# Element-wise work of a streaming encoder step moved from GpSimd to VectorE

## The chip, the cores and the metric

One core of one Trainium2 chip. The metric is device time in microseconds of the whole program, from launch to end; lower is better. A core has five engines with queues of their own, each working in order: TensorE (PE: matmuls, and PEld: loads of its weights), VectorE (DVE), ScalarE (ACT), GpSimd (POOL) and SyncE (SP, which here only issues DMAs).

## What is computed

One inference step of a two-layer encoder on 512 prompt tokens and 64 sample tokens, in float32, width 1024. Cut to what matters here:

```python
def rmsnorm(x, g):
    return x * rsqrt(mean(x * x, axis=-1) + 1e-6) * g

def trunk_layer(x, ...):
    h = rmsnorm(x, g_mix_norm)
    proj = h @ w_in                       # split into qa ka va | qg kg vg ag rg | cq ckv kr
    o_a = rmsnorm(stick_breaking_attention(qa, ka, va))
    o_b, gla_s = gla_recurrence(qg, kg, vg, log_a, s0)
    o_b = rmsnorm(o_b) * silu(rg)         # the retrieval gate
    o_c = rmsnorm(mla_attention(cq, ckv, kr))
    x = x + concat(o_a, o_b, o_c) @ w_out
    x = x + memory_cross_attention(rmsnorm(x, g_cross_norm), mem_k, mem_v)
    h = rmsnorm(x, g_ffn_norm)
    return x + (silu(h @ w_gate) * (h @ w_up)) @ w_down

...

# gla_recurrence, each block of 16 tokens
S = exp(b_last) * S + kd.T @ v            # the state, 4 heads of 32 x 64
```

## The kernel before

All 576 tokens are worked at once, in five token tiles (four of 128 and one of 64). The residual stream X lies transposed in SBUF, eight blocks of 128 features by 576 tokens. Each float32 matmul is made of three with split operands: a high part (wH, hH; written by ScalarE) and a low part (wL, hL; value minus high part, written by VectorE). Most operations go through one recording helper, so in the profile they all have line 209, and instructions are told apart by the tiles that they write and read. Tile names carry the stage: `win` the input projection, `gla` gated attention, `sb` stick-breaking attention, `wout` the output projection, `cross`, `ffn`; the digit is the layer.

**The stream's norms** (class `XNorm`, line 480 on). `add(k)` is called once for each of the eight feature blocks, right behind the residual add that completes the block: ScalarE writes hH, VectorE hL, ScalarE the square of the block into a tile of tag `u` (three buffers), and the square of block k is added to the running sum. Seven adds make one norm; those of k = 1 to 6 are on GpSimd, that of k = 7 on VectorE. `add` is called in `wout` (both layers, for the cross attention's norm) and in `down` at the end of the feed-forward block of layer 0 (for the second layer's first norm). A matmul with a constant matrix then sums over features, and ScalarE makes the factor R of it. The norm of layer 0's first stage is computed otherwise.

**The masked values of gated attention** (`states` in `gla`). The update of the state over blocks of 16 tokens is made with matmuls whose right side holds the values of a head once for each of up to eight blocks, zero outside the block: `vm[token, block, :] = vg[token, :] * blk[token, block]`. For each token tile two head pairs are done, each in a buffer of tag `pt` (two buffers): the first head's product on GpSimd, the second one's on VectorE, then four matmuls of TensorE for the pair into accumulator `gla.S`. The fifth tile has 64 tokens and four blocks, so its products are 64x256 instead of 128x512. When all five tiles are in, `scans` runs eight scans on VectorE over the prompt's states (`gla.U`) and one over the sample's.

**The retrieval gate** (`ev` in `win`). VectorE scales the projection out of the accumulator by R into G, ScalarE takes its sigmoid, and GpSimd multiplies G by it; four times in a layer (two feature blocks by two token halves).

The order of the tasks of the mixer stage is written out by hand (`STEPS`): in each layer it says when a unit of the input projection (W), of the states (l), of the scans (m) and so on is emitted. The cross attention's tasks are ordered by a planner with costs for each engine, and the feed-forward block is in program order. From the emitted program, the framework's scheduler makes each engine's queue, taking what comes earlier in the program first as far as its own model has it ready. After that the queues are fixed.

Of the kernel before, what the change touches and what calls it, by code (L numbers as in the profile page):

```python
# [26 lines left out]
KD = D // 128  # L27
# [203 lines left out]
def tile_hybrid(ctx, tc, ins, outs):  # L231
    clock = tc.clock = Clock()
    nc = Engines(tc)
# [16 lines left out]
    def nm(s):  # L250
        uid[0] += 1
        return f"{phase[0]}.{s}_{uid[0]}"

    def big(dt=F32, name="b"):
        return clock.tile(bp.tile([128, BIGN], dt, tag="big", name=nm(name)), "big", 11)

    def big4(dt=F32, name="b"):
        return big(dt, name).rearrange("p (a t) -> p a t", t=T)
# [13 lines left out]
    def u(tag="u", name=None):  # L272
        pool = up if tag in ("u", "R") else turn["pool"]
        return clock.tile(pool.tile([128, T], F32, tag=tag, name=nm(name or tag), bufs=UB[tag]), tag, UB[tag])
# [11 lines left out]
    def ps_(tag):  # L286
        return clock.tile(pp.tile([128, 512], F32, tag=tag, name=nm(tag), bufs=PB[tag]), tag, PB[tag])

    def cst(shape, name, dt=F32):
        return const.tile(shape, dt, tag=name, name=name)  # L290
# [6 lines left out]
    def act(out, in_, func, **kw):  # L297
        name = TABLES.get(func)
        if name is not None and name != held["set"]:
            load = nc.scalar.preload_act_table_set(name).ins  # L300
            for i in held["users"]:
                behind(tc, load, i)
            held.update(set=name, load=load, users=[load])
        ins = nc.scalar.activation(out, in_, func, **kw).ins
        if name is not None:
            behind(tc, ins, held["load"])
            held["users"].append(ins)
# [7 lines left out]
    def tt(out, a, b, op, eng=None):  # L315
        (eng or nc.vector).tensor_tensor(out, a, b, op=op)
# [4 lines left out]
    MUL, ADD, SUB = ALU.mult, ALU.add, ALU.subtract  # L321
# [55 lines left out]
    blk = cst([128, 8], "blk")  # L377
# [34 lines left out]
    def load_w(src, kt, n, src2=None, by="m"):  # L412
        return split_w(fetch_w(src, kt, n, src2), by)
# [38 lines left out]
    def ws_steps(w, m0, kt, aH, aL, evac, halves=(0, 1), tag="D"):  # L452

        ph = phase[0]
        for a in halves:
            phase[0] = ph
            cs = slice(a * HF, (a + 1) * HF)
            d = ps_(tag)[:, 0:HF]
            for k in range(kt):
                mm3(d, w[0](k, m0, m0 + 128), w[1](k, m0, m0 + 128), aH(k)[:, cs], aL(k)[:, cs], k == 0, k == kt - 1)  # L460
            evac(a, cs, d)
            yield "d"
# [17 lines left out]
    class XNorm:  # L480
# [13 lines left out]
        def add(self, k):  # L494
            self.split(k, slice(0, T))
            s = u()
            act(s, X[:, k, :], AF.Square)
            if k:
                tt(s, s, self.acc, ADD, None if k == KD - 1 else nc.gpsimd)
            self.acc = s  # L500

        @property
# [433 lines left out]
    def layer(l, xn):  # L936
# [11 lines left out]
        def nat(c0, n, fn, fn2=None, c1=None, n1=0):  # L948

            w = load_w(wi[:, c0:c0 + n], KD, n, None if c1 is None else wi[:, c1:c1 + n1], by="k")  # L950
            n += n1
            for t, (r0, rn) in enumerate(TILES):
                ps = ps_("D")[:, 0:n]
                for k in range(KD):
                    mm3(ps[0:rn], xn.h(k)[:, r0:r0 + rn], xn.l(k)[:, r0:r0 + rn], w[0](k, 0, n), w[1](k, 0, n),
                        k == 0, k == KD - 1)
                x = fn(t, r0, rn, ps[0:rn])
                if fn2 is not None:
                    od.later(lambda a=(t, r0, rn, x): fn2(*a))
                yield "d"  # L960
# [90 lines left out]
        def win():  # L1051

            G = st["G"] = big4(name="G")
            vgx = st["vgx"] = big(name="vg")
            st["vg"] = vgx[:, 0:1280].rearrange("p (t c) -> p t c", c=256)
            st["vga"] = vgx[:, 1280:1360].rearrange("p (t c) -> p t c", c=16)
            st["ckv"] = vgx[:, 1360:2160].rearrange("p (t c) -> p t c", c=160)
            st["lat"] = big(F32R, name="lat")[:, 0:2176].rearrange("p (a t) -> p a t", t=1088)
            st["krn"] = turn["pool"].tile([128, 288], F32, tag="krn", name=nm("krn"), bufs=1).rearrange("p (t c) -> p t c", c=32)
            w = load_w(wi[:, 768:1024], KD, 256) if l else w_first  # L1060
            for a in range(2):
                for p in range(2):
                    yield from ws_steps(w, p * 128, KD, xn.h, xn.l,
                                        lambda a, cs, d: tt(G[:, p, cs], d, xn.R[:, cs], MUL), [a])

            yield from nat(1808, 160, ckv1, lambda t, r0, rn, ln: lat_T(ln, rn, r0), 1200, 96)
            od.event("qk")
            yield from nat(1024, 256, vg1)
            od.event("vg")
            od.add(lat_past(), name="S")  # L1070
            w = load_w(wi[:, 0:256], KD, 256)
            for p in range(2):
                yield from ws_steps(w, p * 128, KD, xn.h, xn.l, lambda a, cs, d: tt(oSB[p][:, cs], d, xn.R[:, cs], MUL))
            od.add(sb_past(), name="Z")
            w = load_w(wi[:, 256:512], KD, 256)
            for a in range(2):
                for p in range(2):
                    yield from ws_steps(w, p * 128, KD, xn.h, xn.l,
                                        lambda a, cs, d: tt(sbk[:, p, cs], d, xn.R[:, cs], MUL), [a])
                for t in ([0, 1], [2, 3, 4])[a]:  # L1080
                    od.later(lambda t=t: ka_out(t, *TILES[t]))
            yield from nat(512, 256, va1)
            od.event("va")
            yield "after glan"
            w = load_w(wi[:, 1296:1552], KD, 256)
            for p in range(2):
                def ev(a, cs, d):
                    tt(G[:, 2 + p, cs], d, xn.R[:, cs], MUL)
                    s = u()[:, 0:HF]
                    act(s, G[:, 2 + p, cs], AF.Sigmoid)  # L1090
                    tt(G[:, 2 + p, cs], G[:, 2 + p, cs], s, MUL, nc.gpsimd)
                yield from ws_steps(w, p * 128, KD, xn.h, xn.l, ev)
            od.event("rg")
            yield "after glan"
            st["cT"] = big4(F32R, name="cT")
            yield from nat(1552, 256, cq1, cq2)
            od.event("win")
# [194 lines left out]
        def gla():  # L1292
            G, vgx, vg, vga = (st[x] for x in ("G", "vgx", "vg", "vga"))
# [19 lines left out]
            for a in range(2):  # L1313
                cs = slice(a * HF, (a + 1) * HF)
# [20 lines left out]
            for h in range(4):  # L1335
                s = slice(32 * h, 32 * h + 32)
# [10 lines left out]
            def states(t, r0, rn):  # L1347

                if t == 0:
                    st["Uf"] = big(name="U")[:, 0:2112]  # L1350
                    st["U"] = st["Uf"].rearrange("p (d n) -> p d n", n=33)
                    nc.vector.memset(st["U"][:, :, 0:1], 0.0)
                nb = rn // 16
                pt = ps_("T")
                tr(pt[0:rn, 0:128], kdT[:, r0:r0 + rn])
                kd = u()[0:rn, 0:128]
                copyA(kd, pt[0:rn, 0:128])
                yield "S"
                ps = ps_("S")
                for hp in range(2):  # L1360
                    vm = pt4("vm").rearrange("p (h n d) -> p h n d", h=2, n=8)
                    for hh in range(2):
                        h = 2 * hp + hh
                        tt(vm[0:rn, hh, 0:nb, :], vg[0:rn, t, h * 64:h * 64 + 64].unsqueeze(1).broadcast_to([rn, nb, 64]),
                           blk[0:rn, 0:nb].unsqueeze(2).broadcast_to([rn, nb, 64]), MUL, nc.vector if hh else nc.gpsimd)
                    if hp:
                        clock.keep(ps)
                    yield
                    for hh in range(2):
                        h = 2 * hp + hh  # L1370
                        nc.tensor.matmul(ps[32 * h:32 * h + 32, 0:nb * 64], lhsT=kd[:, 32 * h:32 * h + 32],
                                         rhs=vm[0:rn, hh, 0:nb, :].rearrange("p n d -> p (n d)"), start=True, stop=True,
                                         tile_position=(0, 32 * h))
                src = ps[:, 0:nb * 64].rearrange("p (n d) -> p d n", d=64)
                copyA(st["U"][:, :, 1 + 8 * t:9 + 8 * t] if t < 4 else Us[:, :, 1:5], src)
# [461 lines left out]
```

## Time and profile before

| what | value |
|---|---|
| time before, median of 3 runs | 1680.31 us (1679.86 to 1680.92) |
| the profiled execution, its own time | 1681.31 us |
| its span, first to last instruction | 1679.5 us |
| granted TensorE clock, mean | 0.991 |
| TensorE busy | 1644.6 us (98%) |
| VectorE busy | 1208.1 us (72%) |
| ScalarE busy | 898.3 us (53%) |
| GpSimd busy | 213.1 us (13%) |

Busy shares are means over stages with different limits. An engine's idle time before an instruction is put down to what released that instruction; in the timeline it stands in brackets. The granted clock is a share of full speed: 1.00 is 2.4 GHz, 0.50 is 1.2 GHz. Ends of matmuls are modelled, and spans on GpSimd are rough.

### The profile page before, as it was taken

The numbers are of one execution on the slowest core, as the hardware profiler recorded it, in microseconds if no ns is written. First come the engines' busy times: TensorE is split into PE (matmuls) and PEld (weight loads), VectorE is DVE, ScalarE is ACT, GpSimd is POOL, SyncE is SP. The second block draws the span as 40 slices with busy tenths as digits, with TensorE's granted clock in tenths as the row PEclk, the third lists the DMA queues.
The fourth block names the chain that finished last, engine by engine and source line by source line (L and its number), as shares of the span: only waits on it lengthen the run. The fifth ranks groups of instructions, "written<-read, shape, count | busy, mean of one in ns | idle before, by whom it ended". The sixth has DMA issues, their size and how long they took to land.

```text
span 1679.5 us, 30904 instructions
## 1 busy us (share of the span) xinstructions
PE 1644.6 (98%) x12279; PEld 1537.0 (92%) x12279; DVE 1208.1 (72%) x2462; ACT 898.3 (53%) x1915; POOL 213.1 (13%) x303
## 2 busy tenths in 40 slices
PE   8999999999999999999999999999999999999998
PEld 7879788689999999999998889877999999999998
DVE  5746798875898777667567378988668877667663
ACT  6426688755664444344443467886566544344431
POOL 3323341020000000000134043400200000000000
PEclk9999999999999999999999999999999999999999
DMA  5312230022122232322223213201211332322221
GB/s 167 116 45 87 70 108 32 26 76 76 51 76 87 90 98 79 101 82 95 80 71 99 78 54 108 75 27 37 90 52 51 101 101 76 101 83 94 94 83 57
DMA packets 113648, 133.31 MB, mean 79 GB/s; under 512 B 10610, under 2 KB 95712, under 8 KB 113504
## 3 DMA queue, kind: packets, MB, share of 16 engines
q1 hardware_dynamic: 113120, 131.30, 24.6%
q8 instruction: 97, 1.59, 0.4%
q14 instruction: 47, 0.39, 0.1%
q0 software_dynamic: 352, 0.03, 0.0%
q10 hardware_dynamic: 32, 0.01, 0.0%
HBM read 123.64 MB, written 7.68 MB: 78 GB/s over the span
## 4 chain that ended last, share of the span: by engine, by line
PE 78%; DVE 10%; issue 4%; ACT 3%; POOL 2%; DMA 2%; POOLq 0%; ACTq 0%; DVEq 0%
PE ffn0.D L209 9%; PE ffn1.D L209 9%; PE ffn0.T L209 7%; PE ffn1.T L209 7%; PE ffn0.S L209 7%; PE ffn1.S L209 6%; PE win1.D L209 5%; PE win0.D L209 3%; PE wout1.D L209 2%; PE wout0.D L209 2%; PE cross1.D L209 2%; PE cross0.D L209 2%; PE cross0.T L209 1%; PE cross1.T L209 1%; PE mlap0.T L209 1%
## 5 line engine op out<-in xcount | busy, mean ns | idle before, releaser
L209 ACT ACTIVATE ffn1.wH<-ffn1.wraw 128x1024 fp32r<-128x1024 f32 x64 | 59.3, 927 | 116.5 <-PE ffn1.T L209 61.1
L209 ACT ACTIVATE ffn0.wH<-ffn0.wraw 128x1024 fp32r<-128x1024 f32 x64 | 59.3, 927 | 111.8 <-PE ffn0.T L209 60.7
L209 DVE TENSOR_TENSOR ffn0.sL<-ffn0.sum,ffn0.sH 128x1024 fp32r<-128x1024 f32 x40 | 48.8, 1221 | 39.7 <-ACT ffn0.sH L209 39.7
L209 DVE TENSOR_TENSOR ffn1.sL<-ffn1.sum,ffn1.sH 128x1024 fp32r<-128x1024 f32 x40 | 48.9, 1221 | 39.7 <-ACT ffn1.sH L209 39.6
L209 DVE TENSOR_TENSOR ffn0.wL<-ffn0.wraw,ffn0.wH 128x1024 fp32r<-128x1024 f32 x64 | 67.5, 1055 | 8.3 <-ACT ffn0.wH L209 7.6
L209 DVE TENSOR_TENSOR ffn1.wL<-ffn1.wraw,ffn1.wH 128x1024 fp32r<-128x1024 f32 x64 | 67.5, 1055 | 8.3 <-ACT ffn1.wH L209 7.6
L209 POOL TENSOR_TENSOR ffn0.u<-ffn0.u,ffn0.u 128x576 f32<-128x576 f32 x6 | 10.0, 1673 | 460.6 <-DVE ffn0.wL L209 453.6
L209 PE MATMUL ffn1.D<-ffn1.bT,ffn1.sH 128*128 128x288 f32 x320 | 65.3, 295 | 0.1
L209 PE MATMUL ffn0.D<-ffn0.bT,ffn0.sH 128*128 128x288 f32 x320 | 65.1, 295 | 0.2
L209 ACT ACTIVATE ffn0.sH<-ffn0.sum 128x1024 fp32r<-128x1024 f32 x40 | 42.2, 1055 | 21.1 <-PE ffn0.S L209 20.9
L209 ACT ACTIVATE ffn1.sH<-ffn1.sum 128x1024 fp32r<-128x1024 f32 x40 | 42.2, 1055 | 21.1 <-PE ffn1.S L209 20.9
L209 PEld LDWEIGHTS ffn0.D<-ffn0.bT,ffn0.sH 128*128 128x128 f32 x320 | 51.6, 189 | 0.9 <-ACT ffn0.part L209 0.9
L209 PEld LDWEIGHTS ffn1.D<-ffn1.bT,ffn1.sH 128*128 128x128 f32 x320 | 51.6, 189 | 0.8 <-ACT ffn1.part L209 0.4
L209 PE MATMUL win0.D<-win0.wH,in.hH 128*128 128x256 f32 (+1 forms) x160 | 47.8, 299 | 0.0
L209 PE MATMUL ffn0.D<-ffn0.bT,ffn0.sL 128*128 128x288 f32 x160 | 47.5, 297 | 0.0
L209 PE MATMUL ffn1.D<-ffn1.bT,ffn1.sL 128*128 128x288 f32 x160 | 47.5, 297 | 0.0
L209 PE MATMUL win0.D<-win0.wL,in.hH 128*128 128x256 f32 (+1 forms) x160 | 46.8, 292 | 0.3 <-DVE win0.wL L209 0.3
L209 PE MATMUL win1.D<-win1.wH,ffn0.hH 128*128 128x256 f32 (+1 forms) x160 | 46.7, 292 | 0.0
L209 PE MATMUL win0.D<-win0.wH,in.hL 128*128 128x256 f32 (+1 forms) x160 | 46.6, 291 | 0.0
L209 PE MATMUL win1.D<-win1.wL,ffn0.hH 128*128 128x256 f32 (+1 forms) x160 | 45.5, 285 | 0.4 <-DVE win1.wL L209 0.4
L209 PE MATMUL win1.D<-win1.wH,ffn0.hL 128*128 128x256 f32 (+1 forms) x160 | 45.4, 284 | 0.0
L209 ACT ACTIVATE ffn1.part<-ffn1.D 128x288 f32<-128x288 f32 x60 | 24.5, 409 | 38.8 <-PE ffn1.D L209 38.8
(977 smaller groups left out, 6590.3 us busy)
## 6 DMA issues: line engine op xcount, KB each, us to landing
ffn0.wraw<-in_w_gate_dram SPq DMA_DIRECT2D x11, 1024.0 KB, 5.3
ffn0.wraw<-in_w_up_dram SPq DMA_DIRECT2D x11, 1024.0 KB, 5.3
ffn0.wraw<-in_w_down_dram SPq DMA_DIRECT2D x11, 1024.0 KB, 5.0
ffn1.wraw<-in_w_gate_dram SPq DMA_DIRECT2D x11, 1024.0 KB, 5.3
ffn1.wraw<-in_w_up_dram SPq DMA_DIRECT2D x11, 1024.0 KB, 5.4
ffn1.wraw<-in_w_down_dram SPq DMA_DIRECT2D x11, 1024.0 KB, 5.0
win1.wraw<-in_w_in_dram SPq DMA_DIRECT2D x7, 1024.0 KB, 5.4
win0.wraw<-in_w_in_dram SPq DMA_DIRECT2D x6, 1024.0 KB, 5.4
```

Source lines behind the costliest of these rows:

```text
L209: r = fn(*args, **kw)
```

## The change

Three calls lose their engine argument, so that the operation goes to the helper's default, VectorE (`tt` takes `eng or nc.vector`): the adds of squares for k = 1 to 6, the gate's multiply, and the first head's masked values of each pair. Nothing else differs; the same operations on the same tiles stand at the same places of the program.

```diff
@@ -496,7 +496,7 @@
             s = u()
             act(s, X[:, k, :], AF.Square)
             if k:
-                tt(s, s, self.acc, ADD, None if k == KD - 1 else nc.gpsimd)
+                tt(s, s, self.acc, ADD)
             self.acc = s
 
         @property
@@ -1088,7 +1088,7 @@
                     tt(G[:, 2 + p, cs], d, xn.R[:, cs], MUL)
                     s = u()[:, 0:HF]
                     act(s, G[:, 2 + p, cs], AF.Sigmoid)
-                    tt(G[:, 2 + p, cs], G[:, 2 + p, cs], s, MUL, nc.gpsimd)
+                    tt(G[:, 2 + p, cs], G[:, 2 + p, cs], s, MUL)
                 yield from ws_steps(w, p * 128, KD, xn.h, xn.l, ev)
             od.event("rg")
             yield "after glan"
@@ -1362,7 +1362,7 @@
                     for hh in range(2):
                         h = 2 * hp + hh
                         tt(vm[0:rn, hh, 0:nb, :], vg[0:rn, t, h * 64:h * 64 + 64].unsqueeze(1).broadcast_to([rn, nb, 64]),
-                           blk[0:rn, 0:nb].unsqueeze(2).broadcast_to([rn, nb, 64]), MUL, nc.vector if hh else nc.gpsimd)
+                           blk[0:rn, 0:nb].unsqueeze(2).broadcast_to([rn, nb, 64]), MUL)
                     if hp:
                         clock.keep(ps)
                     yield
```

## Rows read from the trace of the kernel before

**Rows 1.** Page, part 1: busy time, share of the span, instructions of TensorE.

```profile
PE 1644.6 (98%) x12279; PEld 1537.0 (92%) x12279; DVE 1208.1 (72%) x2462; ACT 898.3 (53%) x1915; POOL 213.1 (13%) x303
```

**Rows 2.** List of waits, TensorE: waited for; us in total, times, longest.

```profile
PE gla0.S L209 <- POOL gla0.vm L209: 2.4, 1, 2.4
...
PE wout0.D L209 <- DVE X L209: 2.3, 2, 2.1
...
PE win0.T L209 <- DVE win0.vg L209: 0.8, 1, 0.8
```

**Rows 3.** View of tile gla0.vm: duration ns min/median/max, first and last start, forms.

```profile
L209 DVE TENSOR_TENSOR gla0.vm<-win0.vg,blk x10: 419/760/1534, 50.8 to 92.1; 128x512 f32<-128x512 f32 x8, 64x256 f32<-64x256 f32 x2
...
L209 POOL TENSOR_TENSOR gla0.vm<-win0.vg,blk x10: 824/1508/5534, 50.8 to 92.6; 128x512 f32<-128x512 f32 x8, 64x256 f32<-64x256 f32 x2
```

**Rows 4.** Timeline, last tile, layer 0: start us, us, engine, instruction, idle before, releaser.

```profile
91.75 1.17 DVE L209 TENSOR_TENSOR gla0.vm<-win0.vg,blk 64x256 f32<-64x256 f32 x2 [0.85 <-PE gla0.S L209]
...
91.82 6.32 POOL L209 TENSOR_TENSOR gla0.vm<-win0.vg,blk 64x256 f32<-64x256 f32 x2 [1.76 <-PE gla0.S L209]
...
92.85 4.89 DVE L209 TENSOR_TENSOR_SCAN gla0.U<-win0.vg,gla0.U 128x264 f32<-128x264 f32 x8
...
98.01 1.23 DVE L209 TENSOR_TENSOR win0.wL<-win0.wraw,win0.wH 128x1024 fp32r<-128x1024 f32 x1
...
98.20 1.06 PE L209 MATMUL gla0.S<-gla0.vm,gla0.u 64*32 64x256 f32 x4 [2.37 <-POOL gla0.vm L209]
```

**Rows 5.** Groups of VectorE instructions by form: busy us, mean ns, idle before, releaser.

```profile
L209 DVE SCALAR_TENSOR_TENSOR wout0.hL<-X,gT,wout0.hH 128x576 fp32r<-128x576 f32 x8 | 8.9, 1114 | 0.8 <-ACT wout0.hH L209 0.8
...
L209 DVE SCALAR_TENSOR_TENSOR ffn0.hL<-X,gT,ffn0.hH 128x576 fp32r<-128x576 f32 x8 | 6.5, 815 | 3.4 <-ACT ffn0.hH L209 3.4
...
L209 DVE TENSOR_TENSOR cross0.wL<-cross0.wraw,cross0.wH 128x1024 fp32r<-128x1024 f32 x6 | 8.6, 1427 | 1.5 <-ACT cross0.wH L209 1.5
...
L209 DVE TENSOR_TENSOR wout0.wL<-wout0.wraw,wout0.wH 128x1024 fp32r<-128x1024 f32 x16 | 19.5, 1222 | 2.4 <-ACT wout0.wH L209 2.4
```

**Rows 6.** Windows, behind that wait: us; busy PE, PEld, DVE, ACT, POOL; clock, DMA.

```profile
99.00:100.00 1.00, 1.00 (x6) 0.81 (x5) 0.44 (x2) 0.47 (x2) 0.91 (x3) 0.50 0.00 0
```

**Rows 7.** Chain of waits: start us, us, what; a group before, two after.

```profile
87.25 3.16 PE win0.D L209 x24
...
99.88 3.97 PE win0.D L209 x24
...
925.38 4.21 PE win1.D L209 x24
```

**Rows 8.** Timeline, TensorE: state matmuls of the second and fourth tile.

```profile
77.38 1.77 PE L209 MATMUL gla0.S<-gla0.vm,gla0.u 128*32 128x512 f32 x8
...
90.56 1.06 PE L209 MATMUL gla0.S<-gla0.vm,gla0.u 128*32 128x512 f32 x8
```

**Rows 9.** Timeline, VectorE: a two-column operation beside the first masked values.

```profile
51.40 1.00 DVE L209 TENSOR_TENSOR win0.y<-win0.y 64x2 f32<-64x2 f32 x1
```

**Rows 10.** Timeline, output projection, layer 0: GpSimd adds, TensorE's wait, the add on VectorE.

```profile
359.84 7.67 POOL L209 TENSOR_TENSOR wout0.u<-wout0.u,wout0.u 128x576 f32<-128x576 f32 x4 [69.53 <-ACT wout0.u L209]
...
368.54 0.40 PE L209 MATMUL wout0.D<-mlas0.mixH,wout0.wH 128*128 128x288 f32 x1 [2.14 <-DVE X L209]
...
376.45 0.75 DVE L209 TENSOR_TENSOR wout0.u<-wout0.u,wout0.u 128x576 f32<-128x576 f32 x1
```

**Rows 11.** Windows: end of the first feed-forward block; the gate's stretch.

```profile
820.00:848.00 28.00, 27.97 (x211) 27.74 (x210) 18.86 (x30) 14.94 (x21) 10.04 (x6) 1.00 0.27 76
...
140.00:165.00 25.00, 24.58 (x193) 22.57 (x193) 20.72 (x37) 14.88 (x38) 11.51 (x16) 1.00 0.29 93
```

**Rows 12.** Timeline, GpSimd: one gate multiply.

```profile
149.32 1.51 POOL L209 TENSOR_TENSOR win0.G<-win0.G,win0.u 128x288 f32<-128x288 f32 x1 [0.83 <-ACT win0.u L209]
```

**Rows 13.** Chain of waits: matmuls behind the output projection's wait, layers 0 and 1.

```profile
368.54 4.93 PE wout0.D L209 x35
...
1192.45 6.47 PE wout1.D L209 x35
```

## The prediction

> **What bounds the kernel now.** I read the page's engine totals first, then the list of TensorE's waits, and only then the timelines of the places where a wait is long. TensorE (PE) is busy for 98% of the span [rows 1], so almost everything is hidden behind its matmuls and a change off TensorE counts only where TensorE stands still. The list of waits [rows 2] names few such places, and three of them touch instructions that this change moves: in each layer 2.4 us for a masked value that GpSimd (POOL) writes, 2.1 us in the output projection for a residual add on VectorE (DVE), and 0.8 us for a row that VectorE normalises. The 2.4, 2.3 and 0.8 of layer 0 stand there; layer 1 repeats all three. The reader should then look at how long the moved instructions take: the same masked value takes 0.42 to 1.53 us on VectorE and 0.82 to 5.53 us on GpSimd [rows 3], and these spreads are the story. The two engines hold each other up. In the timeline of the last token tile [rows 4] the GpSimd pair lasts until 98.14, just after VectorE's eight scans end at 97.74, and TensorE's four state matmuls start only at 98.20, after 2.37 us of standing still. In the other direction, VectorE's low-part subtraction takes 1114 ns beside the GpSimd adds and 815 ns for the same shape in the feed-forward stage, and its weight split 1427 ns against 1222 ns [rows 5].
>
> **The change part by part.** 46 instructions leave GpSimd for VectorE: 20 masked values (one in each of two head pairs, 5 token tiles, 2 layers), 18 adds of squares (6 in each of the three norms built by that class after the first), and 8 gate multiplies. No DMA is added or moved, and neither SP's queue nor POOL's issues one at these places.
>
> (a) Masked values of the last token tile. All four of a tile now go through VectorE ahead of the scans, because they come first in the program. Each is 64x256, 0.42 us where nothing disturbs it [rows 3], so the scans start at most 2 x 0.42 = 0.84 us later, and TensorE finds its operands when it arrives. The wait of 2.37 us goes in each layer: -4.74 us. What is late next is the evacuation and the weight split that stand behind the scans on VectorE [rows 4]; the split is for the next weight block, one product of 24 matmuls (about 3.2 us) away, so I count nothing for it here and make it a rival.
>
> The rows show that the GpSimd instruction was held through all eight scans. The page "SBUF — State Buffer" of the Trainium skill, section "Who interferes with whom", says that VectorE with two SBUF inputs and a GpSimd instruction that reads SBUF exclude each other for a whole instruction, the first to start winning. By that the value would have got in after one scan of some 0.6 us, TensorE would not have waited, and term (a) would be nothing and the sum -2.7 us with (b) gone as well; the trace agrees on the exclusion and not on its length. Since the wait is on record, that rule gets no chance of its own.
>
> (b) The clock behind that wait. After the standstill the granted clock is 0.50, the 1.2 GHz level, between 99 and 100 us [rows 6], and the 24 matmuls that follow take 3.97 us in layer 0 and 4.21 us in layer 1, where such a group takes 3.16 us before it [rows 7]. If TensorE does not stand still I expect the high level throughout: -(0.81 + 1.05) = -1.86 us. The ends are -1.86 and 0: the low level may as well come for another reason.
>
> (c) Masked values of the second tile. TensorE's eight state matmuls take 1.77 us there, against 1.06 us for as much work elsewhere [rows 8]; it waits inside the group for VectorE's value, which GpSimd had delayed. VectorE will write all four values one after another, no later than now but hardly earlier. I take half of the 0.71 us, -0.35 in each layer, -0.7 us; ends -1.4 and 0.
>
> (d) First tile. Beside the first masked values a two-column operation of VectorE takes 1.00 us [rows 9] and the next one nearly as long; both belong to the chain to the normalised row for which TensorE waits 0.8 us. Without GpSimd they are short, but two more masked values of at most 0.75 us each (the price of the wider add [rows 10]) can stand in front. About equal in the worst order: ends -1.6 and 0, taken -0.8 us for both layers.
>
> (e) Adds of squares in the output projection. Four GpSimd adds run from 359.84 to 367.51, and TensorE waits 2.14 us until 368.54 for the residual add that frees its accumulator [rows 10]. VectorE is the bound in this stretch. It gets back what the adds cost it: 8 x (1.114 - 0.815) = 2.4 us on the subtractions and 6 x (1.427 - 1.222) = 1.2 us on the splits [rows 5], 3.6 us. It takes on four adds of 0.75 us [rows 10] ahead of that residual add, 3.0 us. Net -0.6 us per layer, -1.2 us. The add waits on VectorE for ScalarE's square; behind it stand the residual adds, for which both TensorE's accumulators and ScalarE's next scaling wait. ScalarE is ahead here, so I price that wait at nothing. Two later adds fall where VectorE has idle time. Ends: -4.3 (the whole wait in both layers) and +6.0 (no refund at all).
>
> (f) Adds of squares at the end of the first feed-forward block: 6 x 0.75 = 4.5 us on VectorE, which is busy 18.9 of 28 us there, while TensorE is busy 27.97 of 28 [rows 11]. TensorE's matmuls cover it: 0. Without that cover it would be 4.5 us.
>
> (g) Gate multiplies. The costliest of four in a layer takes 1.51 us on GpSimd [rows 12], with the masks of the following attention behind it in its queue; on VectorE it is at most 0.75 us. The attention's masks start about 1 us sooner, VectorE gets four more instructions. TensorE is busy 24.58 of the 25 us there [rows 11]: 0, ends -1 and +1.
>
> Sum: -4.74 - 1.86 - 0.7 - 0.8 - 1.2 = -9.3 us. The profiled execution took 1681.31 us (its span is 1679.5), 1.00 above the median of the runs shown, 1680.31. 1681.31 - 9.3 = 1672.0, less that 1.00: **1671.0 us**.
>
> **The rivals.** First, the stall only moves. TensorE gets past the last tile 2.4 us earlier and then meets the weight split behind the scans, which will end near 100.1 (98.01 + 1.23 + 0.84 [rows 4]); before, TensorE went on at 99.88. Then (a) and (b) are nothing and 1671.0 + 4.74 + 1.86 = 1677.6 us remains. For it speaks that VectorE is strictly in order there; against it that TensorE never waited for that split and needs it one product later.
>
> Second, slower: VectorE becomes the bound in the output projection. If the long subtractions are not GpSimd's doing, the refund of (e) does not come, the four adds cost 3.0 us in each layer, and the longer standstill costs the clock as well: the 35 matmuls after it took 6.47 us in layer 1 and 4.93 us in layer 0 [rows 13], so 1.5 us more in layer 0. The same order-bound queue would put two masked values of 0.7 us in front of the row of (d), 1.4 us per layer. 6.0 + 1.5 + 2.8 = +10.3 us, against it only the 4.74 of (a): 1680.3 + 5.6 = 1685.9 us. It decides from the point where the refund is below what the adds take, 3.0 us a layer. Against it speak the equal shapes of [rows 5]. The page "Perfetto Trace Analysis" of the Trainium skill, section "Optimizing Scalar/DVE Operations", says that work may be worth handing to GpSimd when VectorE is saturated, though their shared port may spoil it; that would give this rival. In the trace the spoiling is what the rows show.
>
> That the change does not do what it says can be left out: the engine is an argument of each call, and its default is VectorE.
>
> **How the numbers follow.** A measurement of this kernel can tell about 0.2%, 3.4 us, from no change, so faster means below 1676.9. The forecast gets 0.73: (a) alone is over that bound, and it rests on a wait that TensorE's own records show. The moved stall gets 0.17, the VectorE bound 0.10. The forecast's own range goes from all lower ends together, 1680.3 - (4.74 + 1.86 + 1.4 + 1.6 + 4.3 + 1) = 1665.4, and a little more for clock levels that I did not price, 1663.5, up to (a) alone with (g) against it, 1676.6. The range given reaches up over the first rival to no change at all, 1680.5; only the second rival lies outside. Faster 0.73, same 0.17, slower 0.10.
>
> **What would show it.** Right: no TensorE wait on the state matmuls of the last tile, no half clock behind them, masked values of 0.4 to 0.7 us with none above 1, subtractions near 815 ns and splits near 1222 ns in the output projection, a wait there below 2.1 us, and TensorE busy time nearly the span through the end of the feed-forward block. Wrong: a new TensorE wait on the weight split behind the scans; a wait on the residual add above 2.1 us; or TensorE waiting longer for attention's probabilities because VectorE came late to its scans.

## The result, and the profile after

The changed kernel takes **1661.57 us** (median of 5 runs, 1660.62 to 1666.25) against 1680.31 us: 18.7 us less between the medians, ratio 0.9895, 95% interval 0.9883 to 0.9907, which is 17.6 us (15.6 to 19.7). The forecast was 1671.0 us, range 1663.5 to 1680.5. The sign was right, but the gain is about twice the forecast and the median lies below the range.

The profiled execution of the changed kernel is its slowest, 1666.25 us with a mean granted clock of 0.994 (three of the others: 0.996). Between the two profiled executions the difference is therefore 15.0 us of span only. Page, part 1, answers to [rows 1]:

```profile
span 1664.5 us, 30858 instructions
PE 1638.2 (98%) x12279; PEld 1532.3 (92%) x12279; DVE 1216.0 (73%) x2508; ACT 897.1 (54%) x1915; POOL 142.2 (9%) x257
```

TensorE stands still for 1664.5 - 1638.2 = 26.3 us, where it was 1679.5 - 1644.6 = 34.9: 8.6 us of waits are gone. The other 6.4 us are busy time, for the same 12279 instructions. Most of that is the clock: a mean granted clock of 0.991 over 1679.5 us costs 15.1 us of full speed, one of 0.994 over 1664.5 us costs 10.0, so 5.1 us. The forecast had 7.4 us of waits and 1.9 us of clock. By the same estimate the run at the median, with 0.996, has some 8 us of clock.

The list of TensorE's waits in the changed kernel, against [rows 2] (waited for; us in total, times, longest):

```profile
PE win0.T L209 <- DVE sb0.PT L209: 0.9, 1, 0.9
...
PE wout0.D L209 <- DVE X L209: 0.7, 2, 0.5
PE wout1.D L209 <- DVE X L209: 0.7, 2, 0.5
```

No wait on `gla0.vm` and none on `win0.vg` is left, and the one on the residual add is down from 2.3 to 0.7 us. The masked values, as in [rows 3], all on VectorE now and none above 0.69 us (duration in ns, min/median/max):

```profile
L209 DVE TENSOR_TENSOR gla0.vm<-win0.vg,blk x20: 409/684/692, 51.0 to 90.3; 128x512 f32<-128x512 f32 x16, 64x256 f32<-64x256 f32 x4
```

The timeline of the last tile, against [rows 4], VectorE and then TensorE:

```profile
89.33 1.42 DVE L209 TENSOR_TENSOR gla0.vm<-win0.vg,blk 64x256 f32<-64x256 f32 x4 [0.78 <-PE gla0.S L209]
90.68 4.29 DVE L209 TENSOR_TENSOR_SCAN gla0.U<-win0.vg,gla0.U 128x264 f32<-128x264 f32 x7
...
95.86 1.19 DVE L209 TENSOR_TENSOR win0.wL<-win0.wraw,win0.wH 128x1024 fp32r<-128x1024 f32 x1
```

```profile
92.85 0.64 PE L209 MATMUL gla0.S<-gla0.vm,gla0.u 64*32 64x256 f32 x8
```

The eight state matmuls run in one go beside the scans, and the weight split behind the scans, which the first rival feared, holds nobody up.

Granted clock in four windows of the kernel before, in the order of time (us; busy PE, PEld, DVE, ACT, POOL; clock, DMA). They lie behind the waits of the first tile, of the last tile in either layer, and of layer 1's output projection:

```profile
57.20:60.20 3.00, 3.00 (x17) 3.00 (x16) 1.37 (x4) 1.00 (x2) 0.00 (x0) 0.50 0.53 165
98.20:101.20 3.00, 3.00 (x13) 2.19 (x14) 1.87 (x2) 0.77 (x2) 2.00 (x5) 0.50 0.15 20
924.20:927.20 3.00, 3.00 (x15) 2.51 (x12) 1.52 (x2) 0.77 (x2) 1.61 (x5) 0.50 0.22 33
1194.00:1197.00 3.00, 3.00 (x14) 3.00 (x14) 2.16 (x4) 1.50 (x3) 1.73 (x2) 0.50 0.66 188
```

The same view of the changed kernel, at the work of the first two of these, and in the two stretches where its clock is still low:

```profile
57.00:60.00 3.00, 3.00 (x27) 3.00 (x27) 0.87 (x3) 1.14 (x2) 0.00 (x0) 1.00 0.45 130
96.00:99.00 3.00, 3.00 (x27) 3.00 (x27) 3.00 (x4) 1.88 (x4) 2.14 (x2) 1.00 0.05 11
173.50:179.50 6.00, 5.83 (x30) 5.17 (x31) 4.73 (x9) 2.15 (x5) 0.29 (x2) 0.50 0.01 3
993.00:999.00 6.00, 6.00 (x31) 5.34 (x32) 4.51 (x9) 2.33 (x5) 0.08 (x1) 0.50 0.00 0
```

Four stretches at 1.2 GHz have gone with their waits, and 27 matmuls start in 3 us where 17 or 13 did. Those inside the tile attention (173 and 993 us), at the 0.9 us waits on `sb0.PT` and `sb1.PT`, stay.

Where the same matmul starts in the two traces gives the gain place by place: at the first tile 2.3 us in layer 0 (0.8 of wait, 1.5 of clock) and 1.0 us in layer 1, at the second tile 0.3 in each, at the last tile 4.4 and 4.5, in the output projections 1.9 and 3.4; behind the last tile, up to and with the tile attention, it gains nothing in layer 0 and loses 2 us in layer 1, in this execution.

### The profile page after: what moved, and what is told of

Same layout as the page of the kernel before. It is cut to its first block, busy times and chain, and to the rows that moved or that the text cites. A ratio compares the mean times of both kernels' runs of the same rounds, so it can differ in the third digit from the quotient of the medians.

```text
span 1664.5 us, 30858 instructions
## 1 busy us (share of the span) xinstructions
PE 1638.2 (98%) x12279; PEld 1532.3 (92%) x12279; DVE 1216.0 (73%) x2508; ACT 897.1 (54%) x1915; POOL 142.2 (9%) x257
## 4 chain that ended last, share of the span: by engine, by line
PE 81%; DVE 7%; issue 4%; ACT 3%; DMA 2%; POOL 1%; ACTq 0%; POOLq 0%; DVEq 0%
PE ffn0.D L209 10%; PE ffn1.D L209 9%; PE ffn0.T L209 7%; PE ffn0.S L209 7%; PE ffn1.T L209 6%; PE ffn1.S L209 6%; PE win1.D L209 6%; PE win0.D L209 4%; PE wout1.D L209 3%; PE wout0.D L209 3%; PE cross1.D L209 2%; PE cross0.D L209 2%; PE cross0.T L209 1%; PE cross1.T L209 1%; PE mlap0.T L209 1%
## 5 line engine op out<-in xcount | busy, mean ns | idle before, releaser
L209 DVE TENSOR_TENSOR ffn1.sL<-ffn1.sum,ffn1.sH 128x1024 fp32r<-128x1024 f32 x40 | 48.9, 1222 | 40.0 <-ACT ffn1.sH L209 39.9
L209 DVE TENSOR_TENSOR ffn0.sL<-ffn0.sum,ffn0.sH 128x1024 fp32r<-128x1024 f32 x40 | 48.9, 1222 | 39.6 <-ACT ffn0.sH L209 39.5
L209 ACT ACTIVATE ffn0.part<-ffn0.D 128x288 f32<-128x288 f32 x60 | 24.5, 409 | 38.4 <-PE ffn0.D L209 38.4
```

The costliest lines, as they stand in the source:

```text
L209: r = fn(*args, **kw)
```

## The experiments

Each kernel was timed in several rounds beside the kernel before on one chip. A gain is between the medians of such a group. A gain by the ratio is 1 less the ratio, times 1680 us. The two differ by up to 1.5 us, so sums of gains have to be compared in one of them. A number in an expectation that follows no forecast term comes from the comparison just given.

**Each part of the change by itself.** On the kernel before, three kernels:

```diff
# e1_values
- ... MUL, nc.vector if hh else nc.gpsimd)
+ ... MUL)
# e2_adds
- tt(s, s, self.acc, ADD, None if k == KD - 1 else nc.gpsimd)
+ tt(s, s, self.acc, ADD)
# e3_gate
- tt(G[:, 2 + p, cs], G[:, 2 + p, cs], s, MUL, nc.gpsimd)
+ tt(G[:, 2 + p, cs], G[:, 2 + p, cs], s, MUL)
```

> Only the 20 masked values go to VectorE; the adds and the gate stay on GpSimd. The forecast's own terms (a) to (d) say -4.74 - 1.86 - 0.7 - 0.8 = -8.1 us, so 1672.2 us. The reading of the two traces (when the same TensorE matmul starts in the one and in the other) says more: -4.2 and -4.5 at the last tile of layers 0 and 1, -2.3 at the first tile of layer 0 (0.8 of wait and 1.5 of half clock behind it), -1.0 at that of layer 1, -0.3 in each second tile, together -12.6 us, 1667.7 us. The rival in which the stall only moves says -1.5 us, 1678.8 us.

Measured: 1666.63 us against 1679.51, ratio 0.9920 (0.9908 to 0.9932), 12.9 us faster. By the ratio it is 13.4 (11.4 to 15.5). The forecast's 8.1 was too little; the reading of the traces held.

> Only the 18 adds of squares go to VectorE. The forecast's term (e) says -1.2 us, 1679.1 us, by the refund of the longer subtractions less the four adds. The reading of the two traces says that TensorE gains 1.9 us in the output projection of layer 0 and 3.4 us in that of layer 1, where the half clock behind it is gone too: -5.3 us, 1675.0 us. The rival in which VectorE becomes the bound says +7.5 us (four adds of 0.75 us in each of two layers and 1.5 us of half clock), 1687.8 us.

Measured: 1674.77 us against 1679.51, ratio 0.9963 (0.9950 to 0.9976), 4.7 us faster, by the ratio 6.2 (4.0 to 8.4). The forecast had the sign and a quarter of the size; the reading of the traces, 5.3, held.

> Only the 8 gate multiplies go to VectorE. The forecast's term (g) says 0, within 1 us: 1679.3 to 1681.3 us. The reading of the two traces is that the stretch of half clock in the attention that follows grew from 3.4 to 6.8 us in layer 1, where TensorE lost about 2 us, and not in layer 0: if the gate does that, this kernel is up to 2 us slower, 1682.3 us. The third possibility is that the gate lets the masks of the attention start sooner and saves the waits there, 1 us or more faster.

Measured: 1679.70 us against 1679.51, ratio 0.9998 (0.9988 to 1.0008). The gate's multiplies are worth nothing, as forecast; its mean clock differs between 0.988 and 0.994 from run to run, and the time with it (1683.0 to 1674.7 us). Whether the gate lengthens the low stretch in layer 1's attention is open. The stretch is long in this kernel's trace too:

```profile
1006.00:1012.00 6.00, 5.45 (x28) 4.80 (x29) 5.10 (x10) 2.09 (x6) 0.67 (x3) 0.50 0.00 0
```

It is so in 4 of the 5 traces that have the gate on VectorE and the attention's copies as they were, and in 1 of 10 that have the gate on GpSimd. By the interval, this kernel is at most 1.3 us slower than the kernel before. The three parts add up to 17.4 of 18.7 us between medians, by the ratios to 20 of 17.6.

**The masked values, tile by tile.** On the kernel before, with the condition that keeps VectorE changed:

```diff
- MUL, nc.vector if hh else nc.gpsimd)
+ MUL, nc.vector if hh or t == 4 else nc.gpsimd)        # e4_last_tile
+ MUL, nc.vector if hh or t == 0 else nc.gpsimd)        # e5_first_tile
+ MUL, nc.vector if hh or 0 < t < 4 else nc.gpsimd)     # e9_middle_tiles
+ MUL, nc.vector if hh or t in (0, 4) else nc.gpsimd)   # e13_first_and_last
```

> Only the masked values of the last token tile, two in each layer, go to VectorE. The forecast's terms (a) and (b) say -6.6 us, 1673.7 us. The reading of the two traces says -4.2 and -4.5, so -8.7 us, 1671.6 us, as the whole stretch of 3.4 us at the half clock goes and not only the part under one group of 24 matmuls. The rival in which the stall only moves behind the scans says no change, 1680.3 us.

Measured: 1673.23 us against 1679.51, ratio 0.9958 (0.9945 to 0.9971), 6.3 us faster, by the ratio 7.1 (4.9 to 9.2). The sum of (a) and (b), 6.6 us, is met, but the interval just takes in the 8.7 of the traces too. The wait and the low clock are both gone from the last tile, and TensorE gains 4.4 and 4.5 us there in this kernel's trace as well. It loses some of it again, because two other stalls, which had kept the high level in the profiled execution of before, have the low one behind them here: the output projection of layer 0 and the first tile of layer 1. The granted clock of this kernel there:

```profile
364.00:367.00 3.00, 3.00 (x14) 3.00 (x14) 2.16 (x5) 1.64 (x3) 1.62 (x1) 0.50 0.60 168
880.00:882.50 2.50, 2.50 (x13) 2.50 (x13) 1.09 (x3) 0.76 (x1) 0.00 (x0) 0.50 0.60 186
```

That the low clock moved there from the last tile is not shown: in the trace of `e10_adds_end_of_ffn`, below, which keeps the wait of the last tile and the low clock behind it, both places have the low level too.

```profile
368.50:371.50 3.00, 3.00 (x15) 3.00 (x14) 2.16 (x4) 1.56 (x3) 1.68 (x2) 0.50 0.49 177
884.00:887.00 3.00, 3.00 (x16) 3.00 (x15) 1.49 (x3) 0.61 (x1) 0.00 (x0) 0.50 0.63 183
```

> Only the masked values of the first token tile, two in each layer, go to VectorE. The forecast's term (d) says -0.8 us, 1679.5 us against 1680.3. The reading of the two traces says that the whole wait of 0.8 us goes in each layer, and with it the stretch of half clock behind it: -2.3 us in layer 0, and -1.0 in layer 1 where the clock had not fallen, or -2.4 in an execution where it had. So -3.3 to -4.8 us, 1675.5 to 1677.0 us.

Measured: 1678.15 us against 1680.78, ratio 0.9980 (0.9971 to 0.9989): 2.6 us faster between the medians, 3.4 by the ratio (1.8 to 4.9). The forecast's 0.8 is outside.

> Only the masked values of the second, third and fourth token tiles go to VectorE, six in each layer. The forecast's term (c) says -0.7 us for both layers; the reading of the two traces says -0.3 us in each second tile and nothing in the others, so -0.6 us: 1679.7 us against 1680.3. What all the masked values gain together (12.9 us as measured) less the last tile (6.3) and the first (3.4) leaves 3.2 us: if the middle tiles have that by themselves, 1677.1 us; if it is there only when no tile is left on GpSimd, this kernel shows at most the 0.6 us.

Measured: 1678.84 us against 1679.64, ratio 1.0000 (0.9991 to 1.0009). Nothing that can be told from no change.

> Only the masked values of the first and of the last token tile go to VectorE, four in each layer; the middle tiles keep theirs on GpSimd. Alone the last tile gave 6.3 us, the first 3.4 and the middle ones 0, 9.7 together, and all of them at once gave 12.9. If the parts simply add, this kernel gives 9.7 us (1670.6 us against 1680.3). If the rest is the clock, which falls behind whichever stall is left (with one stall gone, the records show the low level at the next one), it gives the whole 12.9 us, 1667.4 us, at a mean clock near 0.995 as with all the values moved, where either tile alone has 0.992 to 0.993.

Measured: 1667.73 us against 1680.36, ratio 0.9926 (0.9913 to 0.9938), 12.6 us faster at a mean clock of 0.995, where the last tile alone had 0.992 and the first 0.993. So the middle tiles are not needed for what all the values give. Whether two stalls taken away together give more than each alone is not shown: by the ratios the two alone give 7.1 and 3.4 us, 10.5 together, and this kernel 12.4 (10.4 to 14.6).

**The adds: refund, cost or order.** In the changed program VectorE's queue has a new order in the output projection: two adds and then three residual adds in a row, and a little later the same again. Three kernels:

```diff
# e10_adds_end_of_ffn, on the kernel before
- tt(s, s, self.acc, ADD, None if k == KD - 1 else nc.gpsimd)
+ tt(s, s, self.acc, ADD, None if k == KD - 1 or self.g0 == 8 else nc.gpsimd)
# e6_no_adds, on the kernel before
-            if k:
-                tt(s, s, self.acc, ADD, None if k == KD - 1 else nc.gpsimd)
+            if k == KD - 1:
+                tt(s, s, self.acc, ADD)
# e7_ghost_adds, on the changed kernel, in the output projections' norms
+                if self.ghost and k < KD - 1:
+                    tt(u("sg"), X[:, k, :], X[:, k, :], ADD, nc.gpsimd)
                 tt(s, s, self.acc, ADD)
```

> Only the six adds of squares at the end of the first feed-forward block go to VectorE; those of the two output projections stay on GpSimd. The forecast's term (f) says 0, since TensorE is busy for 27.97 of 28 us there: 1680.3 us, and then the whole gain of the moved adds (4.7 us) is that of the output projections. If VectorE's 4.5 us more were on the path, 1684.8 us. If GpSimd's silence gave something there too, the gain would be up to the 4.7 us.

Measured: 1679.40 us against 1679.64, ratio 1.0001 (0.9992 to 1.0010). Term (f) holds: TensorE's matmuls cover these adds.

> The adds of squares 1 to 6 are left out in the three norms, on every engine; the seventh stays, so each of these norms is taken over two of its eight squares. If the gain of the moved adds (4.7 us as measured alone) is the refund to VectorE's other instructions, and its own adds cost nothing on the path, this is as fast as moving them: 1674.8 us. If the four adds ahead of the residual adds still cost there, it is faster than that by up to 0.5 us of wait and 1.5 us of clock in each layer, 1671 us. If the gain came from the new order of VectorE's queue (in the changed kernel three residual adds stand together ahead of a split) and not from the refund, this kernel, whose queue has nearly the old order, gains nothing: 1679.5 us.

Measured: 1674.76 us against 1680.78, ratio 0.9965 (0.9955 to 0.9976), where the moved adds have 0.9963. Leaving the adds out is worth no more than moving them, so on VectorE they cost nothing that shows in the time, and an order near the old one does as well as the new.

> The changed kernel, and beside each of its adds of squares 1 to 6 in the two output projections GpSimd adds a chunk of the stream to itself, the same shape, into a tile that nobody reads; VectorE's queue has the order of the changed kernel. If the refund comes from GpSimd being silent, VectorE's subtractions go back to 1.0 to 1.9 us and its splits above 2 us, 3.6 us of VectorE's time in each layer, and with the four adds now on VectorE too TensorE waits 2 to 4 us in each layer: 1661.6 + 4 to 8 us and up to 1.5 us of clock in each layer, 1666 to 1673 us. If the order of the queue is what counts, the time stays at 1661.6 us.

Measured: 1672.34 us against 1680.78, ratio 0.9947 (0.9935 to 0.9960): 10.8 us above the changed kernel between the medians, 8.7 by the ratios. VectorE's groups between 340 and 375 us, first of the changed kernel (busy us, mean ns, idle before):

```profile
L209 DVE SCALAR_TENSOR_TENSOR wout0.hL<-X,gT,wout0.hH 128x576 fp32r<-128x576 f32 x8 | 6.5, 815 | 0.5 <-ACT wout0.hH L209 0.5
L209 DVE TENSOR_TENSOR wout0.u<-wout0.u,wout0.u 128x576 f32<-128x576 f32 x7 | 5.3, 753 | 0.0
L209 DVE TENSOR_TENSOR cross0.wL<-cross0.wraw,cross0.wH 128x1024 fp32r<-128x1024 f32 x4 | 4.9, 1222 | 0.5 <-ACT cross0.wH L209 0.5
...
L209 DVE TENSOR_TENSOR wout0.wL<-wout0.wraw,wout0.wH 128x1024 fp32r<-128x1024 f32 x1 | 1.2, 1226 | 0.0
```

and then of the kernel with the ghost adds:

```profile
L209 DVE SCALAR_TENSOR_TENSOR wout0.hL<-X,gT,wout0.hH 128x576 fp32r<-128x576 f32 x8 | 8.4, 1061 | 0.5 <-ACT wout0.hH L209 0.5
...
L209 DVE TENSOR_TENSOR cross0.wL<-cross0.wraw,cross0.wH 128x1024 fp32r<-128x1024 f32 x3 | 4.9, 1649 | 0.0
...
L209 DVE TENSOR_TENSOR wout0.wL<-wout0.wraw,wout0.wH 128x1024 fp32r<-128x1024 f32 x1 | 2.0, 1966 | 0.0
```

Its list of TensorE's waits has a stall as long as the old one back in both layers, now at the first of the three residual adds behind two adds:

```profile
PE wout1.D L209 <- DVE X L209: 3.6, 3, 2.0
...
PE wout0.D L209 <- DVE X L209: 2.3, 2, 2.0
```

Nobody reads what GpSimd adds here, and VectorE's own queue has the order of the changed kernel. The lengthening comes with GpSimd's adds alone: 8 x (1061 - 815) + 3 x (1649 - 1222) + (1966 - 1226) ns = 4.0 us in layer 0 for six adds, 0.67 us each. That is what an add takes on VectorE from start to start (353.45 to 354.12 us below). Handing such an add to GpSimd gave VectorE nothing back. VectorE's timeline in the changed kernel, at the place of [rows 10], from the last residual adds that both kernels have at the same place of their queues:

```profile
349.58 1.25 DVE L209 TENSOR_TENSOR X<-X,wout0.D 128x288 f32<-128x288 f32 x3 [0.62 <-PE wout0.D L209]
...
353.45 0.75 DVE L209 TENSOR_TENSOR wout0.u<-wout0.u,wout0.u 128x576 f32<-128x576 f32 x1
354.12 0.81 DVE L209 SCALAR_TENSOR_TENSOR wout0.hL<-X,gT,wout0.hH 128x576 fp32r<-128x576 f32 x1
354.85 0.75 DVE L209 TENSOR_TENSOR wout0.u<-wout0.u,wout0.u 128x576 f32<-128x576 f32 x1
355.52 1.18 DVE L209 TENSOR_TENSOR X<-X,wout0.D 128x288 f32<-128x288 f32 x3
...
358.48 0.75 DVE L209 TENSOR_TENSOR wout0.u<-wout0.u,wout0.u 128x576 f32<-128x576 f32 x1
...
359.88 0.75 DVE L209 TENSOR_TENSOR wout0.u<-wout0.u,wout0.u 128x576 f32<-128x576 f32 x1
360.55 1.18 DVE L209 TENSOR_TENSOR X<-X,wout0.D 128x288 f32<-128x288 f32 x3
```

The residual add that TensorE waited for in the kernel before is the first of the pair at 368.04 us below; in the changed kernel it is the first of the three at 360.55. VectorE in the kernel before:

```profile
356.08 1.26 DVE L209 TENSOR_TENSOR X<-X,wout0.D 128x288 f32<-128x288 f32 x3 [0.63 <-PE wout0.D L209]
...
368.04 0.81 DVE L209 TENSOR_TENSOR X<-X,wout0.D 128x288 f32<-128x288 f32 x2
```

TensorE's queue has changed there as well. Four transposes of the cross attention, which came behind the whole output projection in the kernel before (first line), now stand just ahead of the matmul that waits for the residual add at 355.52 (second and third line):

```profile
373.42 0.60 PE L209 MATMUL cross0.T<-ident,cross0.sk 128*128 128x128 f32 x4
```

```profile
354.97 0.60 PE L209 MATMUL cross0.T<-ident,cross0.sk 128*128 128x128 f32 x4
356.02 0.40 PE L209 MATMUL wout0.D<-mlas0.mixH,wout0.wH 128*128 128x288 f32 x1 [0.46 <-DVE X L209]
```

**The masked values: who was late.** On the changed kernel, GpSimd repeats two products of the last tile for nobody:

```diff
+ if t == 4 and not hh:
+     gv = u("sg")[:, 0:512].rearrange("p (n d) -> p n d", n=8)
+     tt(gv[0:rn, 0:nb, :], vm[0:rn, hh, 0:nb, :],
+        blk[0:rn, 0:nb].unsqueeze(2).broadcast_to([rn, nb, 64]), MUL, nc.gpsimd)
```

> The changed kernel, and in the last token tile GpSimd multiplies two of VectorE's masked values by the mask once more, the same shape, into a tile that nobody reads, at the time of VectorE's eight scans. If only GpSimd is held by the scans and not VectorE by GpSimd, the product takes about 5 us on GpSimd, the scans stay at 0.67 us each, TensorE does not wait and the time stays at 1661.6 us: then the old wait was GpSimd's being late alone. If VectorE pays too, the scans or what follows them grow by one or two products of 0.8 us, and with a wait of TensorE and 1.5 us of clock behind it in each layer the time is 1663 to 1666 us.

Measured: 1661.01 us against 1679.64, ratio 0.9893 (0.9880 to 0.9907), as the changed kernel. Both descriptions of VectorE and GpSimd miss. GpSimd's timeline of the two products in layer 0, and then the scans by tile (ns, min/median/max):

```profile
90.07 0.73 POOL L209 TENSOR_TENSOR gla0.sg<-gla0.vm,blk 64x256 f32<-64x256 f32 x1 [33.99 <-DVE gla0.vm L209]
```

```profile
91.69 0.74 POOL L209 TENSOR_TENSOR gla0.sg<-gla0.vm,blk 64x256 f32<-64x256 f32 x1
```

```profile
L209 DVE TENSOR_TENSOR_SCAN gla0.U<-win0.vg,gla0.U x8: 670/671/1043, 91.3 to 96.3; 128x264 f32<-128x264 f32 x8
```

The second product starts among the scans, is done in 0.74 us, and one scan takes 1.04 us for it instead of 0.67. TensorE does not notice. That the stall of before was the lateness of a value that GpSimd had to deliver, and not time lost on VectorE, is read from [rows 2] and [rows 4]: TensorE waited for GpSimd, and the eight scans beside it took 4.89 us, 0.61 each, as the seven above do in the changed kernel. This run did not bring the long product back, so why GpSimd was held stays open.

**Further along the same way.** Three kernels, the first two on the changed one:

```diff
# e8_copies_on_act
-                if b:
-                    nc.vector.tensor_copy(PT[:, b, 0:w], pt[:, 0:w])
-                else:
-                    copyA(PT[:, b, 0:w], pt[:, 0:w])
+                copyA(PT[:, b, 0:w], pt[:, 0:w])
# e11_query_scales
- tt(q3[:, :, 0:64], ..., MUL, nc.gpsimd)
- tt(qf, qf, ..., MUL, nc.gpsimd)
+ tt(q3[:, :, 0:64], ..., MUL)
+ tt(qf, qf, ..., MUL)
# e14_three_places: e13_first_and_last, and
- tt(s, s, self.acc, ADD, None if k == KD - 1 else nc.gpsimd)
+ tt(s, s, self.acc, ADD, None if k == KD - 1 or self.g0 >= 16 else nc.gpsimd)
```

> The changed kernel, and in the two attentions with tiles the second copy of the transposed probabilities goes from VectorE to ScalarE. In the changed kernel TensorE's longest wait that is left behind the first stage is 0.9 us for such a copy, in each layer, and the only stretches of half clock left (6.8 us each in the profiled execution) begin there. If the copy is late because VectorE is strictly in order behind its scans, and the clock falls for that wait, both go: -1.8 us of waits and 1.4 to 3 us of clock in each layer, 1654 to 1657 us. If ScalarE, which has the exponentials of these tiles, is then late itself, the wait only changes its name and the time stays within 2 us of 1661.6 us.

Measured: 1662.21 us against 1680.78, ratio 0.9890 (0.9877 to 0.9904): the changed kernel's. The wait and the low clock behind it did go (mean clock 0.997 to 0.999), but the time came back elsewhere, where was not followed up; one wait, on ScalarE, has grown from 0.7 to 1.5 us:

```profile
PE gla1.T L209 <- ACT gla1.u L209: 1.5, 1, 1.5
```

> The changed kernel, and the 40 multiplies that scale the queries of the latent attention (two for each tile, 128x256 and 128x128, 0.4 to 1.65 us on GpSimd) go from GpSimd to VectorE too. If GpSimd's two-input instructions cost VectorE as much as they save it wherever the two meet, TensorE's wait of 0.6 to 0.7 us for such a product goes in each layer and perhaps a stretch of half clock behind it: -1.3 to -4 us, 1657.5 to 1660.3 us. If VectorE, busy 75.3 of 85 us there, has no room for 20 x 0.4 us more in each layer, TensorE waits for it: up to +8 us in each layer, and 1665 us or more. The forecast's way of pricing (a term only where TensorE's wait names the instruction) says -1.3 us.

Measured: 1676.83 us against 1679.64, ratio 0.9981 (0.9973 to 0.9990), 15.3 us slower than the changed kernel, at the same mean clock, 0.996. The list of waits does not hold this: the wait for the query product only changes its releaser, from 0.6 us on GpSimd to 0.6 us on VectorE. TensorE's busy time grew by 13.5 us (page, part 1):

```profile
PE 1651.7 (98%) x12279; PEld 1534.6 (91%) x12279; DVE 1217.8 (73%) x2548; ACT 896.9 (53%) x1915; POOL 113.4 (7%) x217
```

VectorE's own busy time grew by 1.8 us only. TensorE's matmuls of the latent attention also stand in a new order here. Whether VectorE's load or that order costs the 15 us was not separated and stays open.

> Of the 46 moved instructions only 20 go to VectorE: the masked values of the first and the last token tile (four in each layer) and the adds of squares 1 to 6 in the two output projections. If the whole of the change lies in these three places, this is as fast as the changed kernel, 1661.6 us. If the middle tiles, the end of the feed-forward block or the gate add something once the rest is quiet, it is slower than that by 2 us or more.

Measured: 1660.23 us (1659.35 to 1663.06) against 1680.36, ratio 0.9883 (0.9866 to 0.9901). 20 of the 46 moved instructions bring all of the change; the interval overlaps that of the changed kernel, so it is as fast, not faster.

## Why the prediction was wrong in size

- **(a), the wait at the last tile, 4.7 us: right.** The 2.37 us are gone in each layer, and the split behind the scans is not waited for. The first rival falls.
- **(b), the clock behind it, 1.9 us: mis-sized at its own place.** It counted the low level under one group of 24 matmuls. In the traces the last tile gains 4.4 and 4.5 us, 2.0 and 2.1 beyond the wait, so some 4 us for both layers. That the last tile alone gave 6.3 us, 7.1 by the ratio, where (a) and (b) have 6.6, is partly luck: that kernel's trace has the 4 us too, and loses at two other stalls.
- **(c), the second tile, 0.7 us:** inside its ends. The traces show 0.3 us in each layer, and the three middle tiles alone nothing measurable.
- **(d), the first tile, 0.8 us: mis-sized.** Two more values were to stand in front of the row at worst, so half was taken. In the changed queue one of the four values stands behind the row, TensorE's whole wait of 0.8 us went in both layers, and in layer 0 so did a low clock of 1.5 us behind it that the step had not looked for. 2.6 to 3.4 us as measured alone.
- **(e), the output projection, 1.2 us: mis-sized.** The account of VectorE was right: a refund of 3.6 us was forecast, 4.0 came by the ghost adds, and four adds do stand ahead of that residual add, at 0.67 us from start to start where 0.75 was taken. From the common residual adds on, VectorE reaches it after 360.55 - 349.58 = 10.97 us instead of 368.04 - 356.08 = 11.96, so 1.0 us sooner where 0.6 was forecast. But TensorE gains 1.9 us in layer 0: while it would wait it now does four transposes that it did later before, and 0.5 us of wait is left. And in layer 1 a low clock of 1.5 us is gone as well. Neither was in the step. 4.7 to 6.2 us as measured alone. The second rival, 5.6 us slower, rested on the refund staying away, and falls.
- **(f) and (g):** 0 forecast, and nothing measured that can be told from 0.
- **The clock, priced at one place only.** The failing step under all of these is that (b) charged the low level to the last tile and left the others to "a little more for clock levels that I did not price", 1.9 us. Every stall that is removed takes away its chance of a low stretch. Forecast 1.9 us of clock; by the granted clock 5.1 us between the profiled executions, and some 8 at the median. The waits were forecast at 7.4 us and are 8.6.

The parts moved alone (last tile, first tile, middle tiles, adds) give 6.3, 2.6, 0.8 and 4.7 us between medians, 14.4 together, where the change gives 18.7. By the ratios they give 7.1, 3.4, 0 and 6.2, 16.7 together, where it gives 17.6 (15.6 to 19.7). So it is not shown that the change gives more than its parts.

## What to carry to other kernels

Price a stall of TensorE as its wait plus the stretch of half clock that may follow it, some 1.5 to 2 us here, at every stall that a change removes. A two-input GpSimd instruction beside a busy VectorE saves VectorE nothing if VectorE loses as much by it: compare the lengthening of its neighbours with what the instruction takes on VectorE itself, here 0.67 us against 0.67. But moving all of it over is no rule: the query scales made the kernel 15 us slower, so move what a wait names, and measure.

## What the runs showed of the hardware that was not expected

The low clock follows stalls, but not each of them. Where the first tile of layer 0 still has its wait (7 of the 16 traces), a stretch at 0.50 stands behind it every time; in the 9 traces without the wait, never. Behind the 2 us wait of the output projections it stands in 12 of 18 places (9 traces, two layers), and in none of the 14 places where that wait is gone. The same kernel's time moves with these stretches: the gate kernel took 1674.7 us at a mean clock of 0.994 and 1683.1 us at 0.989.

One product of 64x256 on GpSimd took 5.53 us beside the scans in the kernel before [rows 3], and as long in both layers of the six other kernels that leave it there. It took 0.74 us beside the same scans when its result was for nobody. The Trainium skill, page "SBUF — State Buffer", section "Who interferes with whom", says that whichever of the two engines issues first holds the shared pair for the whole instruction and the other blocks. The 0.74 us, with one scan longer by 0.37 us, agrees with that; the 5.53 us through eight scans does not. In the old case GpSimd started at 92.6 us, while VectorE was inside its own masked value, and in the new one at 91.69 us, while VectorE was inside a scan. The first of the two products for nobody started inside a masked value as well, at 90.07 us, with another masked value behind it and not a scan, and took 0.73 us. So neither the start inside a masked value nor the scans alone hold GpSimd up. The products also read different tiles; what decides was not tried.
